# A hybrid decoder step on one core: the two threshold searches that run side by side share one tile for their candidates and counts

## The chip, the cores and the metric

The kernel runs on one core of a Trainium2 chip. The metric is the device time of one execution in microseconds (us); smaller is better. The core has five engines with an instruction queue each, worked through in order: TensorE (PE in the profile; its weight loads are PEld), VectorE (DVE), ScalarE (ACT), GpSimd (POOL) and SyncE (SP, which here only starts transfers). An instruction waits at the head of its queue until the semaphores that it names are up, and everything behind it in that queue waits too.

## The reference

One layer of a decoder for a prompt of 2048 tokens and for 8 sample tokens with a paged cache of 16384 keys each. In the prompt's sparse attention an indexer gives every (query, key) pair a score, the sum over 8 heads of `relu(iq . ik) * iw`; keys behind the query are masked out, the 256 keys of highest score are kept, and softmax attention reads those alone:

```
scores = where(kpos <= qpos, indexer_scores(iq, iw, ik), -inf)
_, idx = top_k(scores, 256)
att    = softmax_attention(q, k[idx], v[idx], valid = idx <= qpos)
rec    = hgrn2_mixer(...)                     # gated linear recurrence, 4 heads, in chunks
x      = x + concat(att, rec) @ w_out
x      = x + square(relu(rms_norm(x) @ w_up)) @ w_down
```

The sample tokens go through the same layer with a top-256 over their cache pages. Outputs are the two hidden states, the new keys, values and indexer keys, and the recurrence's states, in float32.

## The kernel before

Matrix products are done in three passes (line 126, `mm3`): each float32 operand is split into a high and a low part, and lines 127, 128 and 129 are high*high, high*low and low*high. So PE has most of the work.

The prompt is cut into 16 blocks of 128 queries. The order of the work is: projection (lines 380 to 473), then the recurrence (line 646), beside both of them the indexer (line 477), which writes each block's scores to memory (`scoreD`); then, for three groups of blocks (0 to 4, 5 to 10, 11 to 15 with the sample tokens, line 148), attention (`attend_all`, line 949) and the MLP (`mlp_group`, line 1618).

The **choice** (lines 514 to 593) is what the change touches. Instead of gathering 256 keys, attention adds a mask to dense logits; the choice makes that mask. For one block, a [128, n] tile `S` of scores is loaded (line 588; n is 128 times the block's number plus one, so 384 for block 2 and 2048 for block 15). `search_signs` (line 518) finds the 256th largest score of each row bit by bit, from bit 31 down to 0, in 32 steps. One step is one ScalarE instruction over the whole of `S` that counts, by the sum of signs, how many scores lie above the candidate (line 528; the sum comes out in a [128, 1] tile `cntA`), and two VectorE instructions on [128, 1] tiles: `incA` from the count (line 529) and the next candidate `candA` from `incA` (line 532, in the last step line 534). The next step's count needs that candidate. Then `choose` (line 540) makes the mask on VectorE with about 20 instructions, the long ones over n columns, and stores it (`mbD`); attention loads it at line 974. Blocks 0 and 1 have at most 256 keys and need no search.

`choose_all` (line 294) runs **two lanes**: each takes the next block from the list, and one step of the outer loop advances each lane by one step. The two blocks of a pair have tiles of their own (`candA0`, `candA1`, and so on), and no instruction of one lane waits for the other. There are three places: blocks 2 to 7 beside projection, indexer and recurrence (line 189), blocks 8 to 11 beside the MLP of group 0 (line 241), blocks 12 to 15 beside the MLP of group 1 (line 250). In the MLPs a `Track` (line 273) lets out one step of the outer loop for every 12000 or 14000 columns that PE is given (line 307), while the sample tokens' own key search (line 160, `picks`; lines 1165 to 1526) is let out in the same way.

The order of instructions in each queue is not written by hand. A scheduler with a list of priorities and a model of the engines places every instruction when it expects it to be ready; the priorities are at line 319. So a change in one place can move instructions elsewhere.

Names that return below: `ix` is the PSUM tile of the indexer's products (two buffers, line 498), evicted by ScalarE (line 502) and summed by VectorE into `sl` (lines 504 and 506); `up` and `dn` are the PSUM tiles of the MLP (two and three buffers), evicted by ScalarE (line 1721, `rl`) and by VectorE (line 1748, `y`); `kl`, `rs` and `sc` belong to the sample tokens' search.

Of the kernel before, what the change touches and what calls it, by code (L numbers as in the profile page):

```python
# [8 lines left out]
F32 = mybir.dt.float32  # L9
# [3 lines left out]
I32 = mybir.dt.int32  # L13
# [9 lines left out]
P = 128  # L23
# [22 lines left out]
def hymba_kernel(ctx, tc, x_prompt, x_sample, cache_k, cache_v, cache_kidx, state_hgrn, page_table,  # L46
# [247 lines left out]
    def choose_all(choose_block, blocks):  # L294

        left = [b for b in blocks if TOPK < (b + 1) * P <= SEQ]

        def lane(k):
            while left:
                yield from choose_block(left.pop(0), k)  # L300

        running = [lane(k) for k in range(2)]
        while running:
            running = [x for x in running if next(x, x) is not x]
            yield "choice"

    PACE, PUMP = (12000, 14000), (7000, 9000)
    LATER = 12
# [205 lines left out]
    def choose_keys(px):  # L514
        def small(name, dt=F32, bufs=2):
            return px.tile([P, 1], dt, tag=name, name=name, bufs=bufs)

        def search_signs(b, S, k):


            n = (b + 1) * P
            cand = small(f"candA{k}", I32)
            inc = small(f"incA{k}", I32)
            nc.vector.memset(cand, 0)
            for j in range(31, -1, -1):
                cnt = small(f"cntA{k}")
                jk = px.tile([P, SEQ], I8, tag=f"jkA{k}", name="jkA", bufs=1)
                nc.scalar.activation(jk[:, :n], S[:, :n], AF.Sign, bias=cand.bitcast(F32), scale=-1.0, accum_out=cnt)  # L528
                nc.vector.tensor_scalar(inc, cnt, float(n - 2 * TOPK), -1.0 if j == 31 else float(2 ** j),
                                        op0=OP.is_gt, op1=OP.mult)  # L530
                if j:
                    nc.vector.scalar_tensor_tensor(cand, inc, 1 << (j - 1), cand, op0=OP.bitwise_xor, op1=OP.bitwise_xor)  # L532
                else:
                    nc.vector.tensor_tensor(cand, inc, cand, op=OP.bitwise_xor)
                yield
            return cand.bitcast(F32)
# [45 lines left out]
                nc.vector.tensor_scalar(MB[:, :cn], MB[:, :cn], NEG, None, op0=OP.mult)  # L582
                store(mbD[b, :, s], MB[:, :cn])

        def choose_block(b, k):
            n = (b + 1) * P
            S = px.tile([P, SEQ], F32, tag="S", name="S", bufs=SLOTS)
            nc.sync.dma_start(S[:, :n], scoreD[b, :, :n])
            R = yield from search_signs(b, S, k)
            choose(b, S, R)  # L590
            yield

        return choose_block


    def recurrence(p1, pj):
# [1195 lines left out]
```

## Time and profile before

| what | value |
|---|---|
| median of 3 runs | 3520.95 us (3516.57 to 3522.51) |
| the profiled execution | 3515.95 us, of which the span of the trace is 3514.2 us |
| PE busy | 3315.7 us (94%) |
| DVE, ACT, POOL busy | 2345.8 us (67%), 2202.5 us (63%), 1201.2 us (34%) |
| mean granted clock of PE | 0.977 of full speed |
| search activations (line 528) | 448, 586.3 us of ACT |
| search instructions of DVE (lines 529 and 532) | 448 and 434, 64.2 and 114.5 us |

The page cuts the span into 40 slices, and PE is at 8 to 9 tenths or more in every one of them. Matmuls are pipelined and their ends are modelled, so this is not PE at its peak, but it is the engine that sets the time: what another engine does costs time where PE waits for it. The waits are listed by who released them, and a wait is put down to the semaphore that came last.

### The profile page before, as it was taken

How to read it: one execution, taken by the hardware profiler on the slowest of the kernel's cores; microseconds unless marked ns; L12 is line 12 of the kernel's file. 1: busy time of each engine (PE TensorE's matmuls, PEld its weight loads, DVE VectorE, ACT ScalarE, POOL GpSimd, SP SyncE). 2: the span in 40 equal slices, each digit the busy share in tenths (PEclk: the TensorE clock that was granted, in tenths of full speed). 3: DMA queues.
4: the chain of work that ended last, by engine and by line, in shares of the span. 5: the costliest groups of instructions: out<-in, count | busy, mean ns of one | idle time of the engine just before them, and what ended most of it. 6: DMA issues, size and time to landing. Idle time of an engine off the chain costs nothing. (4 is left out here: it accounts for less than half of the span.)

```text
span 3514.2 us, 56706 instructions
## 1 busy us (share of the span) xinstructions
PE 3315.7 (94%) x20230; PEld 2912.1 (83%) x20230; DVE 2345.8 (67%) x5150; ACT 2202.5 (63%) x4063; POOL 1201.2 (34%) x1460
## 2 busy tenths in 40 slices
PE   8999889999998989989999988999999999999999
PEld 7787788999996778877787778888989788888888
DVE  3577788877684358898795788796384787322323
ACT  5789887777674258858844665765973576333332
POOL 5565776655544035554442101042211000100000
PEclk9999999999999999999999999999999999999999
DMA  6564647464535446555546112334336201444443
GB/s 212 156 177 146 176 144 194 139 165 133 163 104 192 146 133 209 190 170 167 168 148 223 36 59 88 126 100 163 130 127 226 84 25 37 150 144 141 135 136 129
DMA packets 343244, 499.95 MB, mean 142 GB/s; under 512 B 38536, under 2 KB 252144, under 8 KB 341936
## 3 DMA queue, kind: packets, MB, share of 16 engines
q1 hardware_dynamic: 280784, 326.35, 29.4%
q0 software_dynamic: 62176, 169.96, 15.8%
q8 instruction: 159, 2.61, 0.3%
q14 instruction: 125, 1.02, 0.1%
HBM read 374.26 MB, written 121.96 MB: 141 GB/s over the span
## 5 line engine op out<-in xcount | busy, mean ns | idle before, releaser
L528 ACT ACTIVATE jkA<-S,candA 128x1664 int8<-128x1664 f32 (+11 forms) x448 | 586.3, 1310 | 116.8 <-DVE candA L532 101.4
L1748 DVE TENSOR_TENSOR y<-y,dn 128x512 f32<-128x512 f32 x512 | 346.5, 683 | 342.9 <-PE dn L129 339.7
L127 PE MATMUL up<-hh,wh 128*128 128x384 f32 (+2 forms) x1536 | 496.5, 323 | 4.7 <-ACT wh L1570 3.5
L128 PE MATMUL up<-hl,wh 128*128 128x384 f32 (+2 forms) x1536 | 496.2, 323 | 0.0
L129 PE MATMUL up<-hh,wl 128*128 128x384 f32 (+2 forms) x1536 | 491.2, 323 | 4.6 <-DMA wl<-low 3.2
L128 PE MATMUL dn<-dl,uh 128*128 128x512 f32 x1024 | 407.8, 398 | 6.0 <-POOL dl L1574 3.4
L127 PE MATMUL dn<-dh,uh 128*128 128x512 f32 x1024 | 404.5, 399 | 4.8 <-DVE y L1748 4.2
L129 PE MATMUL dn<-dh,ul 128*128 128x512 f32 x1024 | 402.2, 396 | 5.3 <-DVE ul L1724 5.0
L127 PEld LDWEIGHTS up<-hh,wh 128*128 128x128 f32 x1536 | 294.9, 192 | 18.2 <-ACT wh L1570 4.9
L128 PEld LDWEIGHTS up<-hl,wh 128*128 128x128 f32 x1536 | 294.7, 192 | 13.5 <-issue 3.9
L129 PEld LDWEIGHTS up<-hh,wl 128*128 128x128 f32 x1536 | 294.5, 192 | 13.0 <-DMA wl<-low 4.8
L1570 ACT CAST dh<-raw 128x1024 fp32r<-128x1024 f32 x96 | 96.8, 1047 | 284.0 <-PE dn L129 276.7
L129 PEld LDWEIGHTS dn<-dh,ul 128*128 128x128 f32 x1024 | 194.9, 191 | 49.0 <-DVE ul L1724 6.8
L506 DVE SCALAR_TENSOR_TENSOR sl<-ix,iw,sl 128x512 f32<-128x512 f32 (+3 forms) x266 | 180.4, 678 | 78.0 <-ACT ix L502 75.5
L127 PEld LDWEIGHTS dn<-dh,uh 128*128 128x128 f32 x1024 | 193.8, 190 | 42.9 <-DVE y L1748 6.7
L128 PEld LDWEIGHTS dn<-dl,uh 128*128 128x128 f32 x1024 | 195.1, 191 | 38.8 <-POOL dl L1574 4.3
L1724 DVE TENSOR_TENSOR ul<-rl,uh 128x384 fp32r<-128x384 f32 x192 | 114.3, 597 | 157.2 <-ACT uh L1723 155.9
L500 PE MATMUL ix<-IK,iqT 128*128 128x512 f32 (+3 forms) x608 | 187.1, 393 | 28.7 <-DVE sl L506 19.7
L1572 POOL DMA_DIRECT2D dl<-low x64 | 34.9, 545 | 521.9 <-PE dn L129 477.9
L502 ACT ACTIVATE ix<-ix,iw 128x512 f32<-128x512 f32 (+3 forms) x304 | 182.3, 604 | 48.5 <-PE ix L500 45.4
L993 PE MATMUL lg<-KS,aqT 128*128 128x512 f32 (+3 forms) x640 | 195.9, 402 | 14.5 <-DVE mx L995 10.7
L1269 POOL DMA_INDIRECT kg<-in_cache_kidx_dram,pti x128 | 132.3, 1033 | 210.7 <-DVE kt L1271 180.1
(498 smaller groups left out, 9330.6 us busy)
## 6 DMA issues: line engine op xcount, KB each, us to landing
raw<-in_w_up_dram SPq DMA_DIRECT2D x96, 512.0 KB
raw<-in_w_down_dram SPq DMA_DIRECT2D x96, 512.0 KB
wl<-low POOLq DMA_DIRECT2D x72, 512.0 KB
raw<-in_w_in_dram SPq DMA_DIRECT2D x256, 128.0 KB
dl<-low POOLq DMA_DIRECT2D x64, 512.0 KB
wl<-lowp POOLq DMA_DIRECT2D x48, 512.0 KB
low<-wl SPq DMA_DIRECT2D x40, 512.0 KB
low<-dl SPq DMA_DIRECT2D x32, 512.0 KB
```

The source lines that it names most:

```text
L127: nc.tensor.matmul(ps, lh, rh, start=first, stop=False)
L128: nc.tensor.matmul(ps, lh, rl, start=False, stop=False)
L129: nc.tensor.matmul(ps, ll, rh, start=False, stop=last)
L500: nc.tensor.matmul(ps[:, :kn], iqT[:, h], IK[:, i, k0:k0 + kn], start=i == 0, stop=i == 1)
L502: nc.scalar.activation(r[:, :kn], ps[:, :kn], AF.Relu, scale=iw[:, 1, h:h + 1])
L506: nc.vector.scalar_tensor_tensor(sl, r[:, :kn], iw[:, 2, h:h + 1], sl, op0=OP.mult, op1=OP.add)
L528: nc.scalar.activation(jk[:, :n], S[:, :n], AF.Sign, bias=cand.bitcast(F32), scale=-1.0, accum_out=cnt)
L993: nc.tensor.matmul(ps[:, :kn], aqT[:, 2 * u + j], KS[k0 // 512][:, u // 2, i, :kn], start=i == 0, stop=i == 1)
L1269: nc.gpsimd.indirect_dma_start(out=kg_, out_offset=None, in_=kview, in_offset=bass.IndirectOffsetOnAxis(ap=pti[:, b, g, u:u + 1], axis=0))
L1570: nc.scalar.copy(wh, raw)
L1724: nc.vector.tensor_tensor(ul[:, o], rl[:, :cn], uh[:, o].bitcast(F32), op=OP.subtract)
L1748: front["dve"] = nc.vector.tensor_tensor(ys_[t][:, s], ys_[t][:, s], po, op=OP.add)
```

## The change

The two blocks of a pair become one search. `choose_blocks` loads both score tiles and widens the first block's tile by 128 columns, which POOL fills with -3e38 (they count as not above any candidate, so n is the same for both). `search_signs` then has one `candA`, one `incA` and one `cntA` of two columns for the pair: in each step ScalarE counts both blocks, one after the other, each into its column, and VectorE makes both increments in one instruction and both candidates in another. After the 32 steps the two masks are made one after the other, with a step of the outer loop each. `choose_all` takes the blocks in twos. In the new file the activation stands at line 523, the `incA` instruction at 525, the `candA` instruction at 528, the mask's first long instruction at 541 (before: 545) and the fill at 589.

```diff
--- before.py
+++ after.py
@@ -294,15 +294,9 @@
     def choose_all(choose_block, blocks):
 
         left = [b for b in blocks if TOPK < (b + 1) * P <= SEQ]
-
-        def lane(k):
-            while left:
-                yield from choose_block(left.pop(0), k)
-
-        running = [lane(k) for k in range(2)]
-        while running:
-            running = [x for x in running if next(x, x) is not x]
-            yield "choice"
+        for i in range(0, len(left), 2):
+            for _ in choose_block(left[i:i + 2]):
+                yield "choice"
 
     PACE, PUMP = (12000, 14000), (7000, 9000)
     LATER = 12
@@ -515,17 +509,19 @@
         def small(name, dt=F32, bufs=2):
             return px.tile([P, 1], dt, tag=name, name=name, bufs=bufs)
 
-        def search_signs(b, S, k):
-
-
-            n = (b + 1) * P
-            cand = small(f"candA{k}", I32)
-            inc = small(f"incA{k}", I32)
+        def search_signs(n, Ss):
+
+
+            m = len(Ss)
+            cand = px.tile([P, m], I32, tag=f"candA{m}", name="candA", bufs=2)
+            inc = px.tile([P, m], I32, tag=f"incA{m}", name="incA", bufs=2)
             nc.vector.memset(cand, 0)
             for j in range(31, -1, -1):
-                cnt = small(f"cntA{k}")
-                jk = px.tile([P, SEQ], I8, tag=f"jkA{k}", name="jkA", bufs=1)
-                nc.scalar.activation(jk[:, :n], S[:, :n], AF.Sign, bias=cand.bitcast(F32), scale=-1.0, accum_out=cnt)
+                cnt = px.tile([P, m], F32, tag=f"cntA{m}", name="cntA", bufs=2)
+                for k, S in enumerate(Ss):
+                    jk = px.tile([P, SEQ], I8, tag=f"jkA{k}", name="jkA", bufs=1)
+                    nc.scalar.activation(jk[:, :n], S[:, :n], AF.Sign, bias=cand[:, k:k + 1].bitcast(F32), scale=-1.0,
+                                         accum_out=cnt[:, k:k + 1])
                 nc.vector.tensor_scalar(inc, cnt, float(n - 2 * TOPK), -1.0 if j == 31 else float(2 ** j),
                                         op0=OP.is_gt, op1=OP.mult)
                 if j:
@@ -582,15 +578,22 @@
                 nc.vector.tensor_scalar(MB[:, :cn], MB[:, :cn], NEG, None, op0=OP.mult)
                 store(mbD[b, :, s], MB[:, :cn])
 
-        def choose_block(b, k):
-            n = (b + 1) * P
-            S = px.tile([P, SEQ], F32, tag="S", name="S", bufs=SLOTS)
-            nc.sync.dma_start(S[:, :n], scoreD[b, :, :n])
-            R = yield from search_signs(b, S, k)
-            choose(b, S, R)
-            yield
-
-        return choose_block
+        def choose_blocks(blocks):
+            n = (blocks[-1] + 1) * P
+            Ss = []
+            for b in blocks:
+                S = px.tile([P, SEQ], F32, tag="S", name="S", bufs=SLOTS)
+                own = (b + 1) * P
+                nc.sync.dma_start(S[:, :own], scoreD[b, :, :own])
+                if own < n:
+                    nc.gpsimd.memset(S[:, own:n], NEG)
+                Ss.append(S)
+            R = yield from search_signs(n, Ss)
+            for k, b in enumerate(blocks):
+                choose(b, Ss[k], R[:, k:k + 1])
+                yield
+
+        return choose_blocks
 
 
     def recurrence(p1, pj):
```

How the instructions stand on **ScalarE** in the last pair (blocks 14 and 15, beside the MLP of group 1; `rl`, `uh` are the MLP's evictions, `wh`, `dh` its weights). Before:

```order
L528 ACTIVATE jkA,cntA_28663<-S,candA_28299 128x2048
L1721 ACTIVATE rl<-up 128x384
L1570 CAST wh<-raw 128x1024
L528 ACTIVATE jkA,cntA_29051<-S,candA_28289 128x1920
L1722 ACTIVATE rl<-rl 128x384 x2
L528 ACTIVATE jkA,cntA_28706<-S,candA_28299 128x2048
L528 ACTIVATE jkA,cntA_29113<-S,candA_28289 128x1920
L1723 CAST uh<-rl 128x384 x2
L528 ACTIVATE jkA,cntA_28758<-S,candA_28299 128x2048
L528 ACTIVATE jkA,cntA_29189<-S,candA_28289 128x1920
```

And now:

```order
L1724 ACTIVATE rl<-up 128x384
L523 ACTIVATE jkA,cntA<-S,candA 128x2048 x2
L1726 CAST uh<-rl 128x384
L1725 ACTIVATE rl<-rl 128x384
L523 ACTIVATE jkA,cntA<-S,candA 128x2048 x2
L1726 CAST uh<-rl 128x384
L1724 ACTIVATE rl<-up 128x384
L1725 ACTIVATE rl<-rl 128x384
L1726 CAST uh<-rl 128x384
L1724 ACTIVATE rl<-up 128x384
L523 ACTIVATE jkA,cntA<-S,candA 128x2048 x2
```

The two counts of a step now stand together, both over 2048 columns, with other instructions between one step and the next. Over all seven pairs, 200 of the 224 steps have the two counts side by side, and in 13 of the 217 places between one step and the next of a pair nothing else stands.

On **VectorE** in the first pair (blocks 2 and 3, beside the projection), around the end of block 2's mask. Before, where the other lane's search (`incA`, `candA`) goes on:

```order
L574 SCALAR_TENSOR_TENSOR rk<-eq 128x384
L529 TENSOR_SCALAR incA_12568<-cntA_12710 128x1
L565 TENSOR_TENSOR need<-need,ngt 128x1
L360 TENSOR_TENSOR zo<-psp,rh_1725 128x64
L532 SCALAR_TENSOR_TENSOR candA_12567<-incA_12568,candA_12567 128x1
L506 SCALAR_TENSOR_TENSOR sl<-ix,iw,sl 128x128
L566 TENSOR_SCALAR need<-need 128x1
L417 TENSOR_SCALAR zo<-psp 128x8
L579 TENSOR_SCALAR cut<-rk,need 128x384
L581 SCALAR_TENSOR_TENSOR MB<-S,V,cut 128x384
```

And now:

```order
L570 SCALAR_TENSOR_TENSOR rk<-eq 128x384
L354 TENSOR_TENSOR zo<-psp,rh_2390 128x512
L561 TENSOR_TENSOR need<-need,ngt 128x1
L541 TENSOR_SCALAR eq,ngt<-S,candA 128x512
L562 TENSOR_SCALAR need<-need 128x1
L555 TENSOR_SCALAR ge<-ngt 128x1
L575 TENSOR_SCALAR cut<-rk,need 128x384
L556 CAST gei<-ge 128x1
L577 SCALAR_TENSOR_TENSOR MB<-S,V,cut 128x384
```

Block 3's mask begins inside block 2's: the first long instructions of the two masks are 18 rows apart, where they were 121 rows apart; in the pairs 4 and 5, and 6 and 7, they are 20 and 45 rows apart (before 120 and 145). In the two MLPs the distance is about what it was.

## Rows read from the trace of the kernel before

**Rows 1.** Stretches: start:end, length, busy us by engine, clock, DMA share, GB/s.
```profile
106.00:570.00 464.00, 426.68 (x2711) 368.63 (x2710) 344.18 (x886) 401.55 (x924) 295.42 (x366) 0.96 0.59 165
1255.00:1860.00 605.00, 552.88 (x2974) 489.82 (x2973) 522.22 (x994) 434.16 (x750) 295.06 (x210) 0.95 0.53 170
2090.00:2662.00 572.00, 543.30 (x3254) 492.02 (x3253) 426.12 (x988) 388.58 (x531) 112.54 (x151) 0.97 0.39 129
```

**Rows 2.** Lines by form: count, busy us, mean ns, idle before: the search's activation.
```profile
L528 ACT ACTIVATE jkA<-S,candA 128x384 int8<-128x384 f32 x32 | 19.9, 623 | 7.7 <-DVE candA L532 3.7 <-DMA S<-scoreD 2.2 <-DVE incA L529 1.7
L528 ACT ACTIVATE jkA<-S,candA 128x2048 int8<-128x2048 f32 x32 | 63.9, 1997 | 11.3 <-DVE candA L532 11.0 <-DVE need L565 0.3
```

**Rows 3.** Busy us of line 529 on DVE in the same three stretches.
```profile
106.00:570.00 464.00, 28.46 (x192) 0.96 0.59 165
1255.00:1860.00 605.00, 17.49 (x128) 0.95 0.53 170
2090.00:2662.00 572.00, 18.26 (x128) 0.97 0.39 129
```

**Rows 4.** Busy us of line 532 on DVE in the same three stretches.
```profile
106.00:570.00 464.00, 65.15 (x186) 0.96 0.59 165
1255.00:1860.00 605.00, 30.23 (x124) 0.95 0.53 170
2090.00:2662.00 572.00, 19.14 (x124) 0.97 0.39 129
```

**Rows 5.** Waits of PE in 106 to 570 us: releaser, us, times, longest.
```profile
PE ix L500 <- DVE sl L506: 15.8, 13, 3.7
...
PE ix L500 <- DVE need L566: 0.4, 1, 0.4
```

**Rows 6.** Waits of PE in 1255 to 1860 us: releaser, us, times, longest.
```profile
PE sc L1230 <- DVE kl L1283: 11.1, 4, 4.4
...
PE po L127 <- DVE kt L1271: 0.3, 1, 0.3
```

**Rows 7.** Waits of PE in 2090 to 2662 us: releaser, us, times, longest.
```profile
PE tp L1612 <- DVE hn L1680: 5.4, 4, 3.0
...
PE dn L127 <- DVE y L1748: 2.3, 1, 2.3
```

**Rows 8.** Timeline of ACT near 2472 us: start, length, instruction, idle before it.
```profile
2471.73 1.99 ACT L528 ACTIVATE jkA<-S,candA 128x2048 int8<-128x2048 f32 x1
...
2473.72 1.98 ACT L1570 CAST dh<-raw 128x1024 fp32r<-128x1024 f32 x2
...
2491.48 2.00 ACT L528 ACTIVATE jkA<-S,candA 128x2048 int8<-128x2048 f32 x1 [1.46 <-DVE candA L532]
```

**Rows 9.** Timeline of DVE near 2491 us.
```profile
2491.21 0.16 DVE L532 SCALAR_TENSOR_TENSOR candA<-incA,candA 128x1 int32<-128x1 int32 x1
...
2493.61 0.15 DVE L529 TENSOR_SCALAR incA<-cntA 128x1 int32<-128x1 f32 x1 [1.30 <-ACT jkA L528]
2493.80 0.16 DVE L532 SCALAR_TENSOR_TENSOR candA<-incA,candA 128x1 int32<-128x1 int32 x1
```

**Rows 10.** Timeline of DVE at 356 us: a tile of four columns.
```profile
356.49 0.16 DVE L657 TENSOR_TENSOR lmx<-lbt 128x4 f32<-128x4 f32 x1 [2.44 <-DMA lbt<-in_lower_bounds_dram]
```

**Rows 11.** Timeline of PE while the mask of block 6 is made.
```profile
492.92 0.74 PE L500 MATMUL ix<-IK,iqT 128*128 128x512 f32 x2 [1.00 <-DVE sl L504]
...
510.43 1.08 PE L500 MATMUL ix<-IK,iqT 128*128 128x512 f32 x2 [2.29 <-DVE sl L506]
```

**Rows 12.** Busy us in 2500 to 2600 us, all engines.
```profile
2500.00:2600.00 100.00, 100.00 (x507) 91.00 (x506) 57.93 (x140) 90.22 (x114) 11.86 (x17) 1.00 0.39 130
```

**Rows 13.** Busy us in 2500 to 2600 us, line 528 alone (ACT).
```profile
2500.00:2600.00 100.00, 65.40 (x65) 1.00 0.39 130
```

**Rows 14.** Line 976: a small fill on POOL.
```profile
L976 POOL MEMSET MB<- x2: 245/298/350, 611.6 to 611.8; 128x128 bf16 x1, 128x256 bf16 x1
```

**Rows 15.** Line 974: the loads of the masks by attention.
```profile
L974 SPq DMA_DIRECT2D MB<-mbD x14: 319/320/485, 1069.4 to 2862.1; - x14
```

## The prediction

> **What bounds the kernel now.** I read the busy shares over the whole span first, then the same shares for the three stretches in which the choice runs, then the waits of PE in each of them, and last the timelines of ScalarE and VectorE. In the three stretches PE works 426.7 of 464, 552.9 of 605 and 543.3 of 572 us [rows 1]: 37.3, 52.1 and 28.7 us, 118 us together, are all that anything beside PE can give back there, apart from the clock (granted 0.96, 0.95 and 0.97). The reader should see that the three are unlike. In the first, ScalarE is busy 401.6 of 464 us (87%) and VectorE 74%; in the second VectorE is the fullest engine after PE (522.2 of 605, 86%); in the third both have a quarter or more free. Of PE's waits those ended by VectorE matter here: 8 rows in the first stretch, which sum to 28.2 us [rows 5], 11 rows and 44.5 us in the second [rows 6], 5 rows and 21.7 us in the third [rows 7]; the first and the last of each list are shown. The search is off the critical path as such: PE never needs a candidate. It costs time only by standing in front of something that PE needs, in ScalarE's or VectorE's queue.
>
> **The change part by part.**
>
> *Half of the search's VectorE instructions go.* Before there are two per step and block, 2 x 32 x 14 = 896; now 448. Their busy time halves if an instruction over two columns takes as long as one over one: a tile of four columns took 0.16 us [rows 10], the instructions of one column 0.15 and 0.16 us [rows 9]. So what goes is (28.46 + 65.15)/2 = 46.8 us in the first stretch, (17.49 + 30.23)/2 = 23.9 in the second and (18.26 + 19.14)/2 = 18.7 in the third [rows 3, 4], which is 13.6%, 4.6% and 4.4% of VectorE's busy time there [rows 1]. If PE's waits for VectorE shrink by the same shares, PE gets back 28.2 x 0.136 + 44.5 x 0.046 + 21.7 x 0.044 = 3.8 + 2.0 + 1.0 = 6.8 us. I take that; the bounds are 0 (the waits belong to long instructions, not to these) and 25.6 us (worked out under the first rival).
>
> The Trainium skill speaks against this term: its page "Perfetto Trace Analysis", section "Optimizing Scalar/DVE Operations", says that grouping helps where the engine is saturated, and that where it is not, but makes others wait, instructions are better broken up. The trace bears out its condition, since VectorE has 14 to 26% free in all three stretches. By that rule the term is 0; I weigh it as the fourth rival.
>
> *ScalarE counts 128 columns more for the smaller block.* The activation took 623 ns over 384 columns and 1997 ns over 2048 [rows 2], so (1997 - 623)/13 = 106 ns for 128 columns, and with 32 steps in 7 pairs 23.7 us: 10.1 in the first stretch, 6.8 in each other. ScalarE has 62, 171 and 183 us free there [rows 1], and that hides it. Where the cover is thin, in the first stretch, PE's products `ix` go through ScalarE to VectorE; 10.1 of 401.6 us is 2.5%, and 2.5% of the 28.2 us is 0.7. I take +1, with bounds 0 and +10.1.
>
> *Both counts must be in before either candidate moves.* That is the wait the change adds. Without a queue, the round trip from the end of a count to the start of the next is 0.59 us: 0.13 from the count's end (2491.48 + 2.00 [rows 8]) to `incA` at 2493.61, 0.19 to the start of `candA`, 0.16 for it [rows 9], and 0.11 from the end of `candA` at 2491.37 to the count at 2491.48 [rows 8, 9]. Before, the other lane's count (1.99 us from start to start [rows 8]) covered it. Now the cover is whatever the order has between two steps, and it has something in all but 13 of 217 places, as the change's section says. 13 x 0.59 = 7.7 us of ScalarE's time is left bare. Behind the waiting count stand the MLP's evictions (`rl`, `uh`) and weight casts, and PE waits for those; but ScalarE has slack, so I take +1 of it, with bounds 0 and +7.7 (the case where the cover fails is the third rival).
>
> *Two counts now stand back to back*, so an eviction can come 2 x 1.99 = 4.0 us late [rows 8]. The order of before has such doublets too in the last pair, and PE worked 100 of 100 us in the middle of it [rows 12]. I take 0; the bounds are 0 and +6, a tenth of a microsecond or two for each of the 32 steps.
>
> *Seven fills of 128 columns on POOL.* The nearest row is a fill of 0.25 to 0.35 us [rows 14], together 2.5 us on an engine with 169 us and more free in each stretch. A fill waits until the mask before has let go of its tile, and behind it in POOL's queue stand the sample tokens' gathers and the subtractions of the weights; I take 0, with bounds 0 and +5.
>
> *One more step of the outer loop per pair* (34 for 33). In an MLP that is 12000 or 14000 columns of PE each, so the last mask is let out some 10 us later. In the first stretch the search also ends later, as block 2 now waits for block 3's scores. The masks are read from 1069.4 us on [rows 15], and the first stretch ends at 570: 0.
>
> The sum is -6.8 + 1 + 1 = -4.8 us, say -5, so 3515.95 - 5 = 3511 for an execution like the profiled one (span 3514.2 plus 1.75 around it). The profiled execution lies 5.0 us under the median of the runs; the same -5 on the median gives **3516 us**. That is 0.14%, and what a measurement of this kernel can tell from no change is about 0.2%, or 7 us.
>
> **The rivals.**
>
> First, *VectorE's queue thins out and the waits shrink more than in proportion.* If a wait grows as u/(1-u) with the busy share u, the first stretch goes from 0.742 to 0.641 (waits down 38%), the second from 0.863 to 0.824 (26%), the third from 0.745 to 0.712 (15%): 10.7 + 11.6 + 3.3 = 25.6 us, less the 2 of ScalarE, -24: 3497. For it: the longest waits in the first stretch are for `sl`, whose instruction stands among those of the search [rows 5]. Against: the second stretch's longest waits are for `kl` [rows 6], a few at a time, and an order made anew need not keep its gaps.
>
> Second, *slower: the two masks of a pair meet on VectorE.* While block 6's mask was made, PE waited five times for VectorE between 492.9 and 510.4 us, 1.00 to 2.29 us each, 6.7 us together [rows 11]; the mask's long instructions stood in front of `sl`. Now the masks of a pair begin 18 to 45 rows apart instead of 120 to 145. If each of the three early pairs pays for one such meeting, it is 3 x 6.7 = 20 us, less the 5: +15, or 3536. It decides from the point where VectorE cannot return `sl` within the two `ix` buffers. Against: during the two masks no search runs, so VectorE and ScalarE are emptier just then.
>
> Third, *slower: ScalarE becomes the bound in the last pair.* In 2500 to 2600 us ScalarE is busy 90.2 us, 65.4 of it line 528 with 32.5 counts and as many readouts, so 16.25 steps of 6.15 us, and 24.8/16.25 = 1.53 us of other work per step [rows 12, 13]. Now a step takes 2 x 1.99 + 1.53 + 0.59 = 6.10 us even if nothing covers the round trip, just under 6.15; but if VectorE's queue makes the round trip 1.46 us, as in the wait shown [rows 8], it is 6.97, and 32 x 0.82 = 26 us less 5 is +21: 3542. PE at 100% in this place speaks for it; the instructions that stand between two steps speak against.
>
> Fourth, *nothing is gained by grouping*: the waits of PE hang on long instructions, and only the two ScalarE terms remain, +2: 3523. For it: the waits that the trace puts down to the search itself are too small to head any of the three lists.
>
> **How the numbers follow.** Forecast 0.40 (its own range 3510 to 3523, since the scheduler places everything anew and some of it falls either way), first rival 0.20, second 0.17, third 0.11, fourth 0.12. Of the forecast I count 0.14 as more than 7 us faster and 0.26 as no change. Faster: 0.14 + 0.20 = 0.34; same: 0.26 + 0.12 = 0.38; slower: 0.17 + 0.11 = 0.28. The range runs from 3494, a little under the first rival, to 3541, which takes in the second and the lower part of the third; about 0.1 lies beyond at the top and 0.05 at the bottom.
>
> **What would show it.** Right: VectorE's busy time falls by about 90 us, lines 529 and 532 having half their count at the old mean; line 528 grows by about 24 us; PE's idle time in the three stretches falls by single microseconds. The first rival shows as waits for `sl` and `kl` that fall by a quarter or more. The second shows as longer waits of PE for `sl` where the masks of blocks 2 to 7 are made; the third as idle time of ScalarE before its counts in the last pair, with PE waiting for `up` evictions. The forecast is wrong if PE's idle time outside the three stretches moves by more than 5 us, for then the new order, and not the search, sets the difference.

## The result and the profile after

The changed kernel takes 3553.87 us (median of 4 runs, 3547.88 to 3555.74) where the kernel before takes 3519.01 us (3516.57 to 3522.51): a ratio of 1.0100 with a 95% interval of 1.0088 to 1.0112. It is 35 us slower, outside the range of the prediction. The profiled execution took 3547.88 us, its span is 3546.2 us.

The busy shares of the three stretches of the choice (moved by the 12 and 22 us that the kernel is late at their starts) come first, as in [rows 1]:

```profile
106.00:570.00 464.00, 428.75 (x2749) 373.42 (x2748) 306.58 (x656) 393.40 (x897) 294.42 (x375) 0.96 0.60 166
1267.00:1872.00 605.00, 549.34 (x2929) 485.49 (x2928) 496.70 (x854) 436.00 (x740) 287.42 (x201) 0.94 0.52 164
2112.00:2684.00 572.00, 541.34 (x3238) 489.19 (x3237) 397.25 (x819) 395.02 (x531) 112.08 (x147) 0.97 0.38 125
```

VectorE (third engine column) is emptier, as forecast, but PE's idle time in the three is 35.3, 55.7 and 30.7 us, against 37.3, 52.1 and 28.7: 3.4 us more in all. Over the whole span the page has PE busy 3315.7 us before and 3327.1 after, so its idle time went from 198.5 to 219.1 us. Most of the 20.6 us lies outside the stretches that I had worked on. The other 11.4 us of the longer span are busy time of PE, for the same 20230 matmuls; the granted mean of its clock fell from 0.977 to 0.970, which goes that way, though no run here separates the clock from the waits.

So I looked at where the two kernels pass the same matmuls. Three first or last starts do: the last `psv` (the recurrence's projections), the first `sc` (the first MLP group's search for sample tokens) and the first `base` (the last of the second attention). Behind the shortest, median and longest duration in ns a row has the first and the last start in us. Before:

```profile
L500 PE MATMUL ix<-IK,iqT x608: 218/394/797, 76.7 to 1055.3; 128*128 128x512 f32 x112, 128*128 128x384 f32 x16, 128*128 128x128 f32 x12, 128*128 128x256 f32 x12
L129 PE MATMUL psv<-wh,hl x544: 274/281/368, 380.4 to 1058.0; 128*128 128x256 f32 x171, 128*8 128x256 f32 x11
L1230 PE MATMUL sc<-kh,BQ x128: 387/394/797, 1277.4 to 1845.1; 128*128 128x512 f32 x128
L1385 PE MATMUL base<-cb,tri x2: 167/174/181, 2254.0 to 2267.2; 128*128 128x8 bf16 x2
```

After:

```profile
L494 PE MATMUL ix<-IK,iqT x608: 219/393/796, 77.5 to 1063.5; 128*128 128x512 f32 x112, 128*128 128x384 f32 x16, 128*128 128x128 f32 x12, 128*128 128x256 f32 x12
L129 PE MATMUL psv<-wh,hl x544: 274/281/561, 375.8 to 1057.5; 128*128 128x256 f32 x171, 128*8 128x256 f32 x11
L1233 PE MATMUL sc<-kh,BQ x128: 387/394/796, 1289.5 to 1863.9; 128*128 128x512 f32 x128
L1388 PE MATMUL base<-cb,tri x2: 166/174/181, 2276.3 to 2289.5; 128*128 128x8 bf16 x2
```

The recurrence's projections end 0.5 us earlier than before. The first `sc` is 12.1 us late and the first `base` 22.3; the end is 31.9 late (the last `dn` starts at 3509.5 before, 3541.4 after). Three losses, then: 12.6 us between the last `psv` and the first `sc`, 10.2 from there to `base`, 9.6 from `base` to the end. None of it is in the first stretch, where six of the fourteen blocks are chosen.

*The first loss.* The scores (`ix`) end 2.7 us before the last `psv` in the kernel before and 6.0 us after it now. The first attention gets the scores' space, and in both traces its first `lg` comes within 4 us of the last `ix`, at 1059.3 and 1064.6 us. In the kernel before it filled the last recurrence head (the `lv` rows): there `lg` and `pt` stand between them. PE of the kernel before, where a bracket is the idle time before a row and what ended it:

```profile
1059.27 0.66 PE L993 MATMUL lg<-KS,aqT 128*128 128x128 f32 x4
1060.34 0.44 PE L993 MATMUL lg<-KS,aqT 128*128 128x128 f32 x2 [0.41 <-DVE mx L995]
1060.62 1.10 PE L808 MATMUL lv<-G 128*128 128x128 f32 x8
...
1061.73 0.30 PE L1016 MATMUL pt<-ident,L 128*128 128x128 f32 x1
```

And of the changed kernel:

```profile
1064.56 0.64 PE L996 MATMUL lg<-KS,aqT 128*128 128x128 f32 x4
1068.62 1.41 PE L811 MATMUL lv<-G 128*128 128x128 f32 x8 [3.42 <-POOL G L799]
1071.89 2.07 PE L811 MATMUL lv<-G 128*128 128x128 f32 x8 [1.86 <-POOL G L799]
1073.76 1.91 PE L811 MATMUL lv<-xq,kk 128*128 128x128 f32 x8
...
1076.67 0.41 PE L1019 MATMUL pt<-ident,L 128*128 128x128 f32 x2
```

PE stands idle for the head's `lv` chain (3.42 and 1.86 us), its granted clock in 1060 to 1080 us is 0.83 on the mean (1.00 before), and the attention's first `pt`, at 1061.7 us before, comes at 1076.7.

*The third loss.* The chain of waits after, at the turn from blocks 12 and 13 to 14 and 15 (start, us, what), holds mask stores, a load of scores and pairs of counts, none of which headed the chain before:

```profile
2432.35 7.83 DMA mbD<-MB
2444.68 4.15 DMA mbD<-MB
2463.89 4.67 DMA mbD<-MB
2472.99 4.89 DMA S<-scoreD
2480.93 4.05 ACT jkA L523 x4
```

The search of the second pair has to wait for both score buffers, and these come free with the two masks. Against [rows 2], ScalarE now sits idle 29.9 us for scores before the counts of blocks 14 and 15 over 2048 columns (in the kernel before 5.3 us, at block 14):

```profile
L523 ACT ACTIVATE jkA<-S,candA 128x2048 int8<-128x2048 f32 x64 | 127.5, 1994 | 33.2 <-DMA S<-scoreD 29.9 <-DVE candA L528 2.7
```

That makes the last mask late, and the last attention stands right behind it. The masks' stores, the loads of masks and the attention's `lg` in the part around it, before (2500 to 2900 us):

```profile
L135 SPq DMA_DIRECT2D mbD<-MB x6: 326/327/333, 2619.1 to 2662.0; - x6
L974 SPq DMA_DIRECT2D MB<-mbD x5: 319/320/320, 2669.0 to 2862.1; - x5
L993 PE MATMUL lg<-KS,aqT x227: 222/397/795, 2735.4 to 2899.9; 128*128 128x512 f32 x92, 128*128 128x128 f32 x8, 128*128 128x256 f32 x8, 128*128 128x384 f32 x6
```

After:

```profile
L135 SPq DMA_DIRECT2D mbD<-MB x6: 319/326/327, 2682.3 to 2724.1; - x6
L977 SPq DMA_DIRECT2D MB<-mbD x5: 319/319/320, 2732.0 to 2892.4; - x5
L996 PE MATMUL lg<-KS,aqT x190: 222/397/795, 2765.6 to 2900.0; 128*128 128x512 f32 x156, 128*128 128x128 f32 x16, 128*128 128x256 f32 x16, 128*128 128x384 f32 x2
```

In both kernels the first load follows the last store by 7 to 8 us, and SyncE's queue waits 6.5 and 7.4 us for that store. Before, the attention's first `lg` came 73.4 us after the store, so the mask had time to spare. Now the last store is 40 us later, counted from `base`, and `lg` comes 41.5 us after it. From `base` to this `lg` it is 489.3 us instead of 481.4: 7.9 of the 9.6 us; from `lg` on the two kernels differ by 1.7.

### The profile page after: what moved, and what is told of

Read it like the earlier page. It is cut to its first block, busy times and chain, and to the rows that moved or that the text cites. A ratio compares the mean times of both kernels' runs of the same rounds, so it can differ in the third digit from the quotient of the medians.

```text
span 3546.2 us, 56301 instructions
## 1 busy us (share of the span) xinstructions
PE 3327.1 (94%) x20230; PEld 2922.0 (82%) x20230; DVE 2294.0 (65%) x4695; ACT 2225.9 (63%) x4063; POOL 1198.3 (34%) x1467
## 5 line engine op out<-in xcount | busy, mean ns | idle before, releaser
L523 ACT ACTIVATE jkA<-S,candA 128x512 int8<-128x512 f32 (+6 forms) x448 | 607.1, 1358 | 111.1 <-DVE candA L528 60.3
L996 PE MATMUL lg<-KS,aqT 128*128 128x512 f32 (+3 forms) x640 | 196.2, 404 | 14.3 <-DVE mx L998 10.9
```

What stands on the lines that cost most here:

```text
L996: nc.tensor.matmul(ps[:, :kn], aqT[:, 2 * u + j], KS[k0 // 512][:, u // 2, i, :kn], start=i == 0, stop=i == 1)
```

## The experiments

Theories: (W) the wider counts and the fills cost it; (C) the common step costs it, that is, a pair starts, moves and ends together; (O) no part of it has this price, but any change to the searches makes the scheduler place scores, recurrence and MLP anew, and the kernel before stands in a good place. Each kernel was timed against the kernel before on the same chip; 1.0000 is its time.

**One part at a time.** Two lanes as before, counts and fill as in the change:

```
-            n = (b + 1) * P
+            n = (b // 2 * 2 + 2) * P
...
+            if b % 2 == 0:
+                nc.gpsimd.memset(S[:, n:n + P], NEG)
```

> The two lanes of the kernel before, each with its own tiles and its own steps; only the smaller block of a pair is now counted over the larger block's columns, with its last 128 columns filled on GpSimd. If ScalarE's 128 more columns per count (23.7 us over the run) and the fill are what cost the 35 us, this takes 3540 to 3555 us. If it is the common step of the two blocks or the order that the scheduler gives the rest, it stays between 3510 and 3527 us, and the score blocks end at the time that they had before (about 1055 us).

3526.13 us, 1.0021 (1.0012 to 1.0031). Six of the 35 us; but the scores end at 1066.3 us, so "at the time that they had before" was wrong. The fill alone:

> The kernel before with only the seven fills of 128 columns added on GpSimd; they write columns that nothing reads, and the counts are as narrow as before. With the counts widened as well it was 3526 us. If the 6 us are ScalarE's wider counts, this stays at 3517 to 3522 us and the scores end at 1052 to 1056 us. If a fill, or any small shift of the order at the start, costs them, it is 3524 to 3529 us and the scores end at 1062 us or later.

3517.27 us, 0.9996 (0.9986 to 1.0006), scores at 1056.3: the fill is free. The common order with own tiles again:

```
-            cand = px.tile([P, m], I32, tag=f"candA{m}", name="candA", bufs=2)
+            cands = [small(f"candA{k}", I32) for k in range(len(Ss))]
```

> The changed kernel with one thing taken back: each block of a pair has its own candidate, increment and count tile again, so a candidate waits for its own count alone, and VectorE has its two instructions per block again (4 per step instead of 2). Common width, fill, common end of the search and masks one step apart stay. If the common tile (both counts before either candidate) costs the time, it returns to 3515 to 3527 us. If the common width, the masks or the order of the rest cost it, it stays at 3545 to 3565 us.

3526.49 us, 1.0018 (1.0008 to 1.0027): what is left is W's 6 us. The scheduler let the lanes run apart again (masks at 195 and 250 us for blocks 2 and 3, as in two lanes). So the common tile carries some 28 us, by one way or another.

**Early and late apart.** `choose_all` takes the common step for `left[0] < AHEAD` or for `left[0] >= AHEAD` only:

> The common step for blocks 2 to 7 alone; blocks 8 to 15, beside the two MLP groups, run in two lanes as before. By the stages of the two traces (the first attention's first score matmul comes 5 us later, the first MLP's 12 us) the early pairs cost 10 to 14 us: 3529 to 3533 us, with the two MLP stages as long as before. If the loss is only where the scheduler happens to put things, the stages after 1290 us change too, though their code is that of the kernel before, by 5 us or more.

3538.34 us, 1.0052 (1.0035 to 1.0070).

> Two lanes for blocks 2 to 7, the common step for blocks 8 to 15 beside the two MLP groups. If each stage has its own cause there, 10 us are lost in the first MLP and 8 in the second: 3536 to 3540 us, and nothing before 1277 us. If the MLPs lose only because the early pairs hand them another order, it stays within 3514 to 3527 us.

3521.57 us, 1.0002 (0.9991 to 1.0014). Early 18, late 1, both 35: the parts don't add up. In both runs it is the branch of the order that held, and not the one of a cause in each stage: with the early pairs alone `sc` to `base` takes 984.0 us instead of 976.6, though its code is that of the kernel before, and the late pairs alone stay within 3514 to 3527 us.

**Width.** Each block over its own columns, increments one by one:

```
+                for k, n in enumerate(ns):
+                    nc.vector.tensor_scalar(inc[:, k:k + 1], cnt[:, k:k + 1], float(n - 2 * TOPK),
```

> The changed kernel with each block counted over its own width again: no more 128 columns, no fill, and VectorE compares the two counts in two instructions, for their thresholds differ (3 per step; the candidates stay one tile). Widening alone cost 6 us on the kernel before (3526 us), and there all of it before 1290 us. If widening is what costs the changed kernel its first 12 us too, this takes 3538 to 3546 us and the scores end at 1055 us; if the common tile holds the rest, it stays above 3535 us. If the loss is order alone, it can land anywhere from 3520 to 3560 us.

3534.48 us, 1.0048 (1.0034 to 1.0063): 19 us better than the change, more than W's 6, but with the scores at 1081.3 us the early loss is still there; the MLP groups gained it.

> As the kernel with the common step for blocks 2 to 7 alone (3538 us), but each block counted over its own width, no fill, three VectorE instructions per step. If the widening is what delays the scores there, it returns to 3516 to 3526 us; if it is the common step (the pair can't start before both its blocks are scored, and its masks come together), it stays at 3533 to 3542 us.

3537.79 us, 1.0057 (1.0038 to 1.0076), as the wide one: W does not explain the early loss.

**Placing.** The two paces 300 columns longer or shorter, the work unchanged:

```
-    PACE, PUMP = (12000, 14000), (7000, 9000)
+    PACE, PUMP = (12300, 14300), (7000, 9000)
```

> The changed kernel with the two paces of the late searches 300 columns longer (12300 and 14300): the same work, put a little elsewhere in the MLP groups. If the 10 and 9 us that the two MLP groups lose belong to the common step, it stays within 5 us of 3554 us. If they come of where the order happens to put things, it moves by more than 5 us, most likely down, towards 3538 us, which is the early pairs' share.

3539.41 us, 1.0062 (1.0041 to 1.0083).

> The changed kernel with the paces 300 columns shorter (11700 and 13700); 300 longer gave 3539 us, the kernel as it is 3554 us. If the 15 us between them are where the order happened to fall, this is nearer to 3539 than to 3554 us (3533 to 3546 us). If a longer pace helps because the common step needs more room in the MLP groups, it is above 3554 us.

3536.47 us, 1.0043 (1.0028 to 1.0057). Both neighbours are 14 to 17 us faster than the change.

> The kernel before with the same two paces (12300 and 14300). It shows how much the placing alone moves a kernel whose work is unchanged: within 4 us of 3520 us if the MLP groups are robust to it, 5 to 15 us above if the paces of before were a lucky place.

3517.28 us, 0.9994 (0.9983 to 1.0005): the kernel before is no lucky pace.

> The changed kernel as it is, once more, beside the same runs of the kernel before. If the time of 3554 us belongs to the program, it is 3549 to 3558 us and its stages repeat within 5 us. If part of the 15 us over its two neighbours with paces 300 columns longer or shorter (3539 and 3536 us) belongs to the chip or the hour, it is below 3547 us.

3551.39 us, 1.0096 (1.0076 to 1.0116). The time belongs to the program: stage by stage the second profile agrees with the first within 3.5 us.

**Starting together.** Own tiles, but both candidates wait for both blocks' scores:

```
-                nc.vector.memset(cand, 0)
+                nc.vector.scalar_tensor_tensor(cand, Ss[0][:, :1], 0.0, Ss[-1][:, :1], op0=OP.mult, op1=OP.mult)
```

> The kernel with own tiles for each block (3526 us), but both candidates of a pair are first set by an instruction that reads both blocks' scores, so that neither search starts before both are there, and none of the next pair before both masks of this one; after that each runs on its own count. If it is this start together that makes the early searches end 88 us later in the changed kernel (the last mask at 662 instead of 574 us) and costs the early 12 us, the last early mask comes at 630 us or later and the time is 3534 to 3545 us. If it is that each step waits for both counts, the mask stays near 590 us and the time at 3523 to 3530 us.

3546.13 us, 1.0082 (1.0065 to 1.0099), just above the range: 20 us over the same kernel without the start. The common tile isn't needed for a loss of this size. But it does not fall where the changed kernel's falls: the last `psv` to the first `sc` takes 244.1 us, 12 more than in the changed kernel, and `base` to the end 1257.4 us, 8 less (the table below), so that the two totals lie 8 us apart is in part chance. How late the early searches end is read from `gei`, one per mask (count, durations, first and last start up to 700 us). Before, after, and this one:

```profile
L560 DVE CAST gei<-ge x6: 140/142/148, 189.3 to 574.2; 128x1 int32<-128x1 f32 x6
```
```profile
L556 DVE CAST gei<-ge x6: 138/142/147, 248.2 to 662.4; 128x1 int32<-128x1 f32 x6
```
```profile
L556 DVE CAST gei<-ge x6: 132/141/145, 243.1 to 653.3; 128x1 int32<-128x1 f32 x6
```

The first mask waits for block 3's scores, each next pair for the two masks before it, and the last mask is 79 to 88 us late.

**More buffers**, so that a pair can be loaded before the masks of the last:

```
-        choose_block = choose_keys(px)
+        choose_block = choose_keys(px, AHEAD * P, 4)
...
+            S = px.tile([P, width], F32, tag="S", name="S", bufs=slots)
```

> The kernel with the common step for blocks 2 to 7 alone (3538 us), with four score buffers of half the width instead of two of full width there (the same space), so that the next pair's scores can be loaded, and its search begun, before the masks of this pair are made. If the wait of a pair for the masks of the one before it delays the early searches, the last early mask comes at 580 to 610 us instead of 664 and the time falls to 3522 to 3530 us. If the early loss is the step itself, or the order, both stay (650 us, 3533 to 3542 us).

3522.2 us, 1.0006 (0.9994 to 1.0017), last mask at 610.3 us, as C said. But the cure is not where C puts it: the first `sc` still stands at 1288.4 us (1293.6 without the buffers), and 11 of the 16 us came between `sc` and `base`, whose code is that of the kernel before.

> The whole changed kernel (3554 us), the common step in all three places, with the one cure that brought the early pairs alone from 3538 to 3522 us: four score buffers of half the width for blocks 2 to 7. If the MLP groups lose only because the early pairs hand them another order (the common step there alone cost 1 us), this takes 3520 to 3530 us. If the common step has its own price of 15 us in the MLP groups once the early one is there, it is 3533 to 3542 us.

3535.48 us, 1.0043 (1.0025 to 1.0060). By the expectation this is a price of the common step in the MLP groups; but the change takes the same 3536 to 3539 us without the buffers where its paces differ, so the run does not tell the two apart.

> The common step for blocks 2 to 7 with four score buffers of half the width (3522 us), each block counted over its own width and no fill. Two lanes lost 6 us by the widening. If that holds here too, it takes 3512 to 3518 us and is faster than both kernels. If the widening costs nothing in the common step (without the four buffers it made no difference, 3538 and 3538 us), it stays at 3518 to 3528 us.

3535.44 us, 1.0038 (1.0023 to 1.0053): outside both ranges and worse than with wide counts. No version of the common step here beats the kernel before.

> The kernel before, its two lanes unchanged, with four score buffers of half the width for blocks 2 to 7. In two lanes a block waits only for the mask of the block two before it, which its own lane has made anyway. If only pairs need the buffers, the time stays at 3515 to 3524 us and the last early mask at 570 to 580 us; if the earlier loads help lanes too, the mask comes 10 us sooner and the time is 3510 to 3516 us.

3551.7 us, 1.0092 (1.0076 to 1.0109). The sharpest miss, outside both ranges: the searches are where they were (first and last mask at 189 and 575 us), yet the last `psv` comes at 1081.3 us, 23 us late. An edit that only allows earlier loads cost as much as the whole change.

**The end of the scores alone.** Twelve head products of block 15's scores are left out, in the changed kernel and in the kernel before (24 of that block's 64 matmuls, so 12 of 32 products; the expectation miscounts them):

```
-                for h in range(NH):
+                for h in range(2 if b == NB - 1 and k0 >= 1024 else NH):
```

> The changed kernel with 12 of the 64 head products of the last block's scores left out (its last 1024 keys are scored by 2 heads instead of 8), so that the scoring ends some 12 us earlier, before the recurrence's last psv matmul; until then the order is that of the changed kernel. If the first 12 us are lost because the scoring outlasts the recurrence's projections and the first attention then starts too late to fill its last head, the stretch from the last psv to the first sc matmul shrinks from 232 to 218 to 222 us, and the time by 12 to 20 us, work left out included: 3534 to 3542 us. If the order of the stretch costs them whatever the scoring does, only the work left out is gained (12 products of 0.6 us): 3545 to 3549 us, and the stretch stays at 228 us or more.

> The kernel before with the same 12 head products left out. Its scoring ends before the last psv matmul in any case, so only the work is gained, 7 us at most: 3512 to 3518 us, and the stretch from the last psv to the first sc matmul stays at 217 to 221 us. If it gains 12 us or more, the comparison with the changed kernel shows nothing.

3541.62 us, 1.0063 (1.0046 to 1.0080), and 3526.64 us, 1.0017 (1.0007 to 1.0028). The changed kernel, cut short:

```profile
L494 PE MATMUL ix<-IK,iqT x584: 219/393/796, 77.4 to 1037.6; 128*128 128x512 f32 x139, 128*128 128x384 f32 x23, 128*128 128x128 f32 x17, 128*128 128x256 f32 x16
L129 PE MATMUL psv<-wh,hl x544: 274/281/561, 375.1 to 1055.1; 128*128 128x256 f32 x171, 128*8 128x256 f32 x11
L1233 PE MATMUL sc<-kh,BQ x128: 387/394/796, 1278.0 to 1858.8; 128*128 128x512 f32 x128
```

From the last `psv` to the first `sc` it is now 222.9 us instead of 232.0: 9 of the 12.6 us of the first loss are gone, and `sc` starts within 0.6 us of the kernel before. Up to 3 of the 9 are the score work itself, four rows of 0.73 us that the changed kernel does behind its last `psv`. The kernel before, cut short, gained nothing and missed both of its ranges: 224.1 us for that stretch, 5 more than before, and 5 us slower in all, for its first MLP was placed anew too. So cut short the two kernels are alike in this stretch, where they were 12.6 us apart.

**All traces side by side** (us, one profiled execution each; "lead" is last `psv` less last `ix`, the stretches as above, "end" being the last `dn`):

| kernel | lead | psv to sc | sc to base | base to end |
|---|---|---|---|---|
| before | 2.7 | 219.4 | 976.6 | 1255.5 |
| fill only | 2.7 | 220.9 | 976.5 | 1252.3 |
| before, other pace | 2.7 | 219.1 | 970.9 | 1259.7 |
| late only | 2.7 | 221.5 | 982.3 | 1266.1 |
| before, four buffers | 4.5 | 218.6 | 987.0 | 1255.1 |
| early only, four buffers, own width | -1.3 | 222.5 | 984.6 | 1254.7 |
| wide | -6.0 | 230.1 | 979.3 | 1249.9 |
| own tiles | -6.1 | 230.9 | 975.8 | 1254.8 |
| early only | -6.0 | 233.7 | 984.0 | 1254.1 |
| after | -6.0 | 232.0 | 986.8 | 1265.1 |
| after, longer pace | -6.0 | 231.5 | 975.7 | 1265.7 |
| after, shorter pace | -6.0 | 233.3 | 980.6 | 1260.2 |
| after, four buffers | -12.9 | 233.2 | 980.7 | 1263.7 |
| early only, four buffers | -13.0 | 233.7 | 972.6 | 1255.7 |
| early only, own width | -14.3 | 232.5 | 984.8 | 1252.1 |
| own width | -14.3 | 231.9 | 972.5 | 1256.6 |
| start together | -31.6 | 244.1 | 983.4 | 1257.4 |

The second column falls in two groups by the sign of the first, 1.3 us beyond zero counting as even: 218.6 to 222.5 (222.9 and 224.1 for the two cut kernels, whose leads are 17 and 28) or 230.1 and more. The third scatters over 16 us without regard to the form: the eight kernels with the common step in that MLP have a mean of 982 (with the cut and the repeated one, which the table leaves out, at 993.5 and 987.2), the ten with two lanes of 980 (with the cut one at 985.4). The fourth differs by form on the mean: common step 1263 of eight, two lanes 1254 of ten; the two kernels with own tiles in a common order are in neither mean. Single kernels overlap, as own width with 1256.6 and the kernel before at its other pace with 1259.7.

What orders the fourth column better than the form is the last mask. Of the nine kernels whose late pairs start together, these are the times of the last mask's store and of the last attention's first `lg`, both counted from `base`:

| kernel | last store | first lg |
|---|---|---|
| start together | 440.4 | 481.0 |
| own width | 441.6 | 481.9 |
| after, shorter pace | 443.5 | 484.2 |
| after, repeated | 446.0 | 486.3 |
| after, cut short | 447.0 | 489.1 |
| after | 447.8 | 489.3 |
| after, four buffers | 448.1 | 489.8 |
| late only | 449.2 | 490.5 |
| after, longer pace | 450.9 | 490.9 |

The two stand in the same order in all nine, and `lg` comes 40 to 42 us behind the store each time. In the eleven kernels whose lanes run apart the store comes at 400 to 411 us and `lg` at 475 to 485, 72 us and more behind it: there the mask does not decide. No run moves the last mask alone, so this rests on the order of the nine.

## Why the prediction was wrong

In short: the terms of the single steps were small, as I took them, but I priced the later end of the searches at nothing. The last mask came late enough to hold up the last attention (some 8 us), scores that ended later left a gap at the end of the recurrence (some 12), and the rest, some 10 us in the first MLP, is where the scheduler happened to put things.

*VectorE's instructions* were halved, and lines 525 and 528 took 66.1 and 50.4 us instead of 64.2 and 114.5: 62 us saved, not 89. In the first stretch 86 increments took 32.0 us where 192 had taken less [rows 3]. The candidate's half came out as forecast (64 us saved, 57 forecast). The increment saved nothing: over two columns it took 169 ns in the median, not 148, and up to 2.54 us (the last section says why). My price for several columns rested on one row of another operation [rows 10].

*PE's waits* for VectorE in the three stretches sum to 26.8, 41.8 and 22.1 us now, against 28.2, 44.5 and 21.7: 3.7 us less where I took 6.8. Long instructions head the lists as in [rows 5, 6]:

```profile
PE ix L494 <- DVE sl L500: 18.7, 12, 4.3
```
```profile
PE sc L1233 <- DVE rs L1241: 14.1, 6, 3.2
PE dn L127 <- DVE y L1751: 8.0, 3, 4.4
```

The waits that the trace puts down to `incA` fell from 5.7 us to 0.3, and others grew. That is nearly the fourth rival's reading: most of the waits belong to long instructions. For an engine that isn't saturated but makes others wait, the Trainium skill ("Perfetto Trace Analysis", "Optimizing Scalar/DVE Operations") speaks for breaking instructions up, which I had read as 0 for this term; the 3.7 us lie between that and my 6.8.

*ScalarE's wider counts.* Its busy time rose by 23.3 us (2202.5 to 2225.9), near the 23.7 forecast. Their price alone was 6 us, within my bounds of 0 to 10.1, not the 1 that I took. *The fills* are free, as said.

*Both counts before either candidate* was priced by the step. No price for it shows: ScalarE's waits for candidates, which it should have lengthened, are shorter, while those for scores, at the start of a pair, went from 9.4 to 42.3 us. The counts' rows of the two pages:

```profile
L528 ACT ACTIVATE jkA<-S,candA 128x1664 int8<-128x1664 f32 (+11 forms) x448 | 586.3, 1310 | 116.8 <-DVE candA L532 101.4
L523 ACT ACTIVATE jkA<-S,candA 128x512 int8<-128x512 f32 (+6 forms) x448 | 607.1, 1358 | 111.1 <-DVE candA L528 60.3
```

*"One more step of the outer loop per pair"* is the step that failed. I named both facts, that block 2 now waits for block 3's scores and that the last mask comes later, by some 10 us in an MLP, and set them to 0 because the masks are read from 1069.4 us on. Two things were wrong in it. The delay was too small: a pair turns as a whole, the next one begins only when both masks have freed both buffers, where two lanes covered each other's turn, and the last mask's store came 40 us later, counted from `base`. ScalarE's longer waits for scores can account for some 25 of these (29.9 less 5.3 us). And 1069.4 us, the first start in [rows 15], is when the first group's attention reads the early masks; there the slack is real. The last attention's first mask load already stood 7.0 us behind the last store before the change, and with the mask 40 us later its `lg` comes 7.9 us later. One reservation stays: the late pairs alone lost 1 us by medians, though their profiled execution (3533.55 us, 12 over their median) shows the longer stretch.

*"The scheduler places everything anew and some of it falls either way"* was worth plus or minus 6 us in my range. It was worth 12 and 10. Where the 12 arise is shown: scores that outlast the recurrence's projections leave its last head without filler, and with the scores cut short the two kernels are alike there. What makes the scores late is not settled. Starting together does it (31.6 us behind the last `psv`), but so do the wider counts in two lanes, and two lanes with other buffers delay the recurrence instead; only edits that leave the early searches' waits and counts as they were (fill, pace, late pairs) keep the lead. The 10 in the first MLP are placing: other paces gave back 6 and 11 of them with the same work, and kernels of both forms lie on either side.

*The rivals.* The first (-24) has half of its sign: the waits for `kl` fell from 11.1 to 7.0 us, but those for `sl` and `rs` rose, and the sum hardly moved. The second named masks that meet on VectorE. Its sign is there, longer waits for `sl` (18.7 us for 15.8), yet up to the last `psv`, where it put its 20 us, the kernel lost nothing. I had also misread [rows 11] for it: of the five waits the shortest is 0.85 us, and two, 2.3 of the 6.7 us, are the recurrence's, for `Sc`. The third had the right place, the last pair, and its sign, ScalarE idle before its counts, but the wrong mechanism: ScalarE was not full but empty, for want of scores. That both late pairs and order would cost at once I gave no chance.

The last sentence of the prediction came true: PE's idle time outside the three stretches rose by 17 us (20.6 less 3.4).

## What to carry to other kernels

Two chains that go side by side hide each other's latency at the ends as well as inside; before joining them, price the turn (last wait of one pair to first work of the next) by buffers and masks, not only the step, and look for each result, not for the first alone, how long before its use it is ready. In a kernel whose order is made by a scheduler, look for the stage that is one transfer or one matmul group from changing its overlap (here scores against recurrence, with 2.7 us to spare), since a small edit elsewhere costs what that overlap is worth. And before believing a loss or a gain of half a per cent, run neighbours that change nothing but the placing: the same change measured 3536, 3539 and 3554 us with three paces.

## What the runs showed of the hardware

Increments of one column took at most 0.17 us in every kernel. In the changed kernel, with two columns, 29 of 224 took over 0.4 us, 32.6 us together, and 28 of these end within 0.15 us of the end of a GpSimd instruction with two inputs; 24 of the short ones overlap such an instruction too. The increment's line (count, shortest/median/longest ns) in the kernel with own widths, and after:

```profile
L526 DVE TENSOR_SCALAR incA<-cntA x448: 107/152/159, 108.7 to 2649.0; 128x1 int32<-128x1 f32 x150
```
```profile
L525 DVE TENSOR_SCALAR incA<-cntA x224: 124/169/2539, 141.1 to 2660.3; 128x2 int32<-128x2 f32 x112
```

One such, from the timelines of VectorE and GpSimd after:

```profile
237.00 1.76 DVE L525 TENSOR_SCALAR incA<-cntA 128x2 int32<-128x2 f32 x1 [3.56 <-ACT jkA L523]
```
```profile
236.34 2.39 POOL L385 TENSOR_TENSOR xt<-xt,g 128x1024 f32<-128x1024 f32 x1 [0.73 <-ACT xt L384]
```

It ends at 238.76 us, with GpSimd's at 238.73. The Trainium skill has the rule ("VectorE: DVE Perf Modes", "What auto-detection actually checks"): an instruction with a single source, source and destination in SBUF and their outermost dimensions (those of 1 left out) both even or equal, takes the two-port mode. The Trainium skill's "GPSIMD Engine Reference", "1. Specifications", says that GpSimd shares its SBUF interfaces with VectorE and contends there with two-port instructions and those with two SBUF inputs. The trace agrees in that two columns were held up and one was not; that the mode was taken no row says. The head's own `E` in the first loss, an instruction with two inputs, goes the same way: 0.42 us at 1040.62 with nothing on GpSimd, 0.95 us at 1061.52 beside GpSimd products over 256 columns, 2.57 us at 1064.50 beside a GpSimd subtraction over 1024.
